# Where the input stage's buffers lie: gather buffers, tables and staging tiles first, the large inputs last

## The chip, the cores and the metric

The kernel runs on one core of a Trainium2 chip. The metric is device time in microseconds (us) of one execution of the whole program, the median of several runs. Lower is better. The engines are TensorE (PE), VectorE (DVE), ScalarE (ACT), GpSimd (POOL) and SyncE (SP, which here only issues DMAs). All of them work out of the on-chip memory SBUF: 128 partitions, in each of which a tile has an address in bytes.

## The reference, cut to what matters

One inference step of a two-layer hybrid decoder, for a prompt of 1024 tokens and eight single-token samples with a paged cache of 4096 rows each. What matters is layer 0: one input projection, whose columns go to a convolution branch and to a sparse attention with three branches, and the sample group's compressed cache, which is a weighted sum of 32 rows a block:

```python
h = x @ w_in                                             # 1032 rows of 1024, all columns
a_val, a_glu, z_a, q, kv6, g3, z_b = jnp.split(h, cuts, axis=-1)
u = a_val * jax.nn.sigmoid(a_glu)
c = lax.conv_general_dilated(ext, conv_w, (1,), 'VALID', ...) + conv_b
ya = jax.nn.silu(_layer_norm(c, cln_g, cln_b)) * jax.nn.silu(z_a)
...
blk = kv_cmp[:, :n_cmp * L_CMP].reshape(B, n_cmp, L_CMP, 2, KV_H, HD_B)   # samples: gathered by page
kc = jnp.einsum('bnlgd,lg->bngd', blk[:, :, :, 0], wk_cmp)
vc = jnp.einsum('bnlgd,lg->bngd', blk[:, :, :, 1], wv_cmp)
...
o = g[..., 0:1] * o_c + g[..., 1:2] * o_s + g[..., 2:3] * o_w   # compressed, selected, window
y = jnp.concatenate([ya, yb], axis=-1) @ w_out
```

Layer 1 is an RWKV-7 recurrence with its own projections, and each layer ends with a layer norm.

## The kernel before

The program has three stages that follow one another on PE.

**The input stage** (`phase_a`, L129, with `conv_norm`, L406) holds the input, 1032 columns by 1024, as a rounded part and a remainder (`xh`, `xl`: "hi" and "lo" parts, so that three fast matmuls stand for one exact one). For each block of 128 projection columns it loads weights `w` (L191, by SP), splits them into `wh` and `wl`, and runs 72 matmuls (L217 to L219). Beside that, as generators that are drawn on in turn, run the convolution and `cmp_task` (L239 to L260): 32 tasks, four for each sample. Each gathers 1 MB of cache pages into one of two buffers `cbuf` by an indirect DMA that POOL issues (L244), with row numbers from the table `cix` (made of `pti`, `ptf` and `cidx`). Three of four then scale the eight rows on ACT by the table `wrow` (L250, eight instructions), add them up on POOL in three steps of 1024, 512 and 256 elements (L252) and add the sum into `acc` on POOL (L253); the fourth does it all on DVE (L258, L260). The last three tasks reach past the last projection matmul. `tmp` (four buffers) stages the input at the start and gate values later; `c` is the convolution's output, `U0` and `U1` its inputs, `cw`, `cvec`, `wcT` and `US` its tables and the samples' states.

**Attention** (`phase_b`, L441) takes the prompt in eight tiles of 128 queries. Two sets of query tiles, `Q[u, 1]` and `Q[u, 2]`, are used in turn. To make a tile, SP loads `qt` (L476) and `zt` (L478), POOL loads two position rows into `Q[u, 2]` (L480), DVE casts the rounded part (L484), ACT copies (L485) and POOL subtracts the remainder (L486); ACT has zeroed part of `Q[u, 2]` once (L466). PE then runs the scores of the compressed (`Kc`), selected (`Ks`) and window (`Kw`) branches (L470), with masks added by a further matmul (L558). The masks `mdiag`, `mfar` come by way of the two staging buffers `PT` (L454, cast at L456), the mask `mcmp` directly (L459). ACT takes the exponentials `Ps` and `Pw` (L567), PE transposes them (L590) and multiplies by the values (L619, L621). The samples' attention (`sample_b`, L746) is worked in between: a cleared tile `QQ` (L764) filled by 16 small copies (L774), transposed compressed keys `KcT` (L808, L811), and 32-column score matmuls (L817).

**The recurrence** is layer 1; its weights, among them `w_out` (L1015), are loaded by SP too.

What sets the order: the code is written in the order of the stages, and a scheduler reorders it for each engine by priority and readiness; it also inserts the waits. Memory is given out by pools: each pool is a contiguous stretch of the partition, and the pools of `phase_a` follow one another in the order in which they are opened. When `phase_a` closes its pools, `phase_b` opens its own over the same bytes. A tile of attention may be written only when the work on all tiles of the input stage that lay under it is over, tile by tile (`reuse_waits="tile"`). So the order of pools in one stage decides what the next stage's tiles wait for. In bytes per partition, from 70,304 on, the input stage lies so: `xh`, `xl` to 136,352; `wh`, `wl` to 152,736; then `c`, the tables, `w`, `U0`, `U1` and more; `tmp` at 187,872; `cbuf` from 204,384 to 220,768. Attention's tiles are, from the same start: the masks to 71,840; the four `Q` tiles 71,872 to 88,256; `PT` to 92,352; `qt` to 96,448; `zt` to 100,544; and on. The samples' tiles come from the other end: `QQ` at 196,736 to 204,928, `KcT` from 207,264.

Of the kernel before, what the change touches and what calls it, by code (L numbers as in the profile page):

```python
# [8 lines left out]
F32 = mybir.dt.float32  # L9
F32R = mybir.dt.float32r  # L10
BF = mybir.dt.bfloat16
I32 = mybir.dt.int32
U32 = mybir.dt.uint32
# [8 lines left out]
NS = 8  # L22
# [3 lines left out]
CW = 31  # L26
# [102 lines left out]
def phase_a(nc, tc, I, O, G, es):  # L129
# [18 lines left out]
    G.acc = kp.tile([128, NS, 4, 64], F32, name="acc")  # L148
    with ExitStack() as ea:
        pool = lambda name, bufs, **k: ea.enter_context(tc.tile_pool(name=name, bufs=bufs, **k))  # L150
        xpl = pool("ax", 1)
        xh = xpl.tile([128, 8, TT], F32R, name="xh")
        xl = xpl.tile([128, 8, TT], F32R, name="xl")
        wp = pool("aw", 2)
        one = pool("a1", 1)
        tp = pool("at", 4)
        cp_ = pool("acmp", 2)
        ps, ps1 = G.ps, G.ps1
        c = one.tile([128, 4, TT], F32, name="c")
        zc = one.tile([64, 1], F32, name="zc")  # L160
# [13 lines left out]
        def build_k(nm, src, w):  # L174
            for g in range(2):
# [2 lines left out]
                nc.scalar.activation(k1[0:64], s, AF.Copy)  # L178
                nc.vector.tensor_copy(k1[64:128], s)
                nc.gpsimd.tensor_tensor(k2[64:128], s, k1[g * 64:g * 64 + 64], op=SUB)  # L180
        cw = one.tile([128, 4, CW], F32, name="cw")
        cwh = cw
        cvec = one.tile([128, 4, 3], F32, name="cvec")
        wcT = one.tile([128, 2, 32], F32, name="wcT")
        US = one.tile([128, 4, NS, CW], F32, name="US")

        def wload(i):
            n = 24 if FM[i][0] == "g3" else 128
# [18 lines left out]
        for i in range(4):  # L207
            nc.sync.dma_start(US[:, i, :, 0:CW - 1], I["conv_state"][:, i])
        nc.vector.tensor_scalar(cwh, cw, 0.5, None, op0=MUL)
# [12 lines left out]

        v2 = lambda t, lo, hi: t[:, lo:hi].rearrange("p (h n) -> p h n", n=NCK)
        U = {}
        pti = one.tile([128, NS], I32, name="pti")
        nc.sync.dma_start(pti, I["pt4"])
        wrow = one.tile([128, 32], F32, name="wrow")
        nc.sync.dma_start(wrow, I["wrow"])
        o, n_ = G.offd["cidx"]
        cidx = one.tile([128, 4], F32, name="cidx")  # L230
        nc.sync.dma_start(cidx, I["cstd"][:, o:o + n_])
        ptf = one.tile([128, NS], F32, name="ptf")
        nc.vector.tensor_copy(ptf, pti)
        nc.vector.tensor_scalar(ptf, ptf, 16.0, None, op0=MUL)
        cix = one.tile([128, NS, 4], U32, name="cix")
        nc.vector.tensor_tensor(cix, ptf.unsqueeze(2).to_broadcast([128, NS, 4]),
                                cidx.unsqueeze(1).to_broadcast([128, NS, 4]), op=ADD)

# [25 lines left out]
        def conv(i, e):  # L264
            u = U[i]
            e.tensor_scalar(c[:, i, 0:T], u[:, 0:T], cwh[:, i, 0:1], cvec[:, i, 0:1], op0=MUL, op1=ADD)
            for k in range(1, CW):
                e.scalar_tensor_tensor(c[:, i, 0:T], u[:, k:k + T], cwh[:, i, k:k + 1], c[:, i, 0:T],  # L268
                                       op0=MUL, op1=ADD)
                yield 1.15  # L270
            nc.scalar.dma_start(O["conv_s"][:, i], US[:, i, :, 1:CW])
            t = tp.tile([128, TT], F32, name="tmp")
            nc.vector.tensor_scalar(t[:, T - CW:T - 1], u[:, T:T + CW - 1], 0.5, None, op0=MUL)
            nc.scalar.dma_start(O["conv_p"][:, i], t[:, T - CW:T - 1])
            tv = t[:, 0:NS * CW].rearrange("p (b k) -> p b k", b=NS)
            nc.vector.tensor_tensor(tv, US[:, i], cw[:, i].unsqueeze(1).to_broadcast([128, NS, CW]), op=MUL)
            nc.vector.reduce_sum(c[:, i, T:TT], tv, axis=AX.X)
            nc.vector.tensor_scalar(c[:, i, T:TT], c[:, i, T:TT], 2.0, cvec[:, i, 0:1], op0=MUL, op1=ADD)
            yield 1.0
# [29 lines left out]
        for i, (kind, j) in enumerate(FM):  # L309
# [14 lines left out]
            if kind == "a":  # L324
# [7 lines left out]
                nc.vector.scalar_tensor_tensor(u[:, CW - 1 + lo:], th[:, lo:T], 1.0, s[:, 0:T - lo], op0=ADD, op1=MUL)  # L332
                nc.vector.scalar_tensor_tensor(US[:, j, :, CW - 1], th[:, T:TT], 1.0, s[:, T - lo:], op0=ADD, op1=MUL)
                nc.vector.tensor_scalar(US[:, j, :, CW - 1], US[:, j, :, CW - 1], 0.5, None, op0=MUL)
                fl.append(conv(j, nc.vector))
# [1515 lines left out]
def body(tc, I, O, stage="all"):  # L1851
# [4 lines left out]
    with ExitStack() as es:  # L1856
# [15 lines left out]
        with ExitStack() as eC:  # L1872
            G.eC = eC
            G.ps = eC.enter_context(tc.tile_pool(name="ps", bufs=2, space=PSUM))
            G.ps1 = eC.enter_context(tc.tile_pool(name="ps1", bufs=1, space=PSUM))
            with ExitStack() as e0:
                G.keepB = e0.enter_context(tc.tile_pool(name="keepB", bufs=1))
                phase_a(nc, tc, I, O, G, e0)
                if stage == "A":
                    nc.sync.dma_start(O["d_ya"], G.scr["ya"])  # L1880
                    nc.sync.dma_start(O["d_zb"][:, :, 0:T], G.scr["zb"][:, :, 0:T])
                    nc.sync.dma_start(O["d_zb"][:, :, T:], G.zs)
                    nc.sync.dma_start(O["d_qc"][:, :, 0:T], G.scr["q"][:, :, 0:T])
                    nc.sync.dma_start(O["d_qc"][:, :, T:], G.qs)
                    return
                phase_b(nc, tc, I, O, G)
                if stage in "BS":
                    nc.sync.dma_start(O["d_zb"], G.scr["yb"])
                    return
            phase_c(nc, tc, I, O, G)  # L1890
# [87 lines left out]
```

## Time and profile before

| | us |
|---|---|
| median of 3 runs | 2210.73 |
| lowest and highest | 2203.44, 2210.95 |
| the profiled execution, its own time | 2201.91 |
| its span, first to last instruction | 2200.2 |
| input stage, to PE's last projection matmul | 0 to 422.8 |
| PE without work between input stage and attention | 422.8 to 446.8 |
| attention on PE | 446.8 to 884 |
| recurrence and end | 884 to 2200 |

The profile is one execution on the chip. Its page gives each engine's busy time; the windows cut the span into stretches and give for each engine the busy time and the number of instructions, PE's granted clock (1.00 is 2.4 GHz, 0.50 is 1.2 GHz) and the share of DMA in use. The timeline lists instructions of one engine in order of start, those of the same kind together ("x3"), and behind them in brackets how long the engine stood idle before and what released it. "PEld" are PE's weight loads, "SPq" is SP's queue of DMA issues.

### The profile page before, as it was taken

How to read it: one execution, taken by the hardware profiler on the slowest of the kernel's cores; microseconds unless marked ns; L12 is line 12 of the kernel's file. 1: busy time of each engine (PE TensorE's matmuls, PEld its weight loads, DVE VectorE, ACT ScalarE, POOL GpSimd, SP SyncE). 2: the span in 40 equal slices, each digit the busy share in tenths (PEclk: the TensorE clock that was granted, in tenths of full speed). 3: DMA queues.
4: the chain of work that ended last, by engine and by line, in shares of the span. 5: the costliest groups of instructions: out<-in, count | busy, mean ns of one | idle time of the engine just before them, and what ended most of it. 6: DMA issues, size and time to landing. Idle time of an engine off the chain costs nothing. (4 is left out here: it accounts for less than half of the span.)

```text
span 2200.2 us, 41365 instructions
## 1 busy us (share of the span) xinstructions
PE 1844.0 (84%) x16026; PEld 1545.8 (70%) x16026; DVE 1491.9 (68%) x2543; ACT 1153.6 (52%) x2359; POOL 972.8 (44%) x784
## 2 busy tenths in 40 slices
PE   5988897668999997897887999897999787987865
PEld 5987896656767886674777987695888666875543
DVE  5998995557788878226364378827748987387453
ACT  3323324544665545357466467747754575465344
POOL 4667667554655545445345212323334434113233
PEclk9998998867999876898898999897899986988956
DMA  6424344521221213546556344433544544353333
GB/s 240 132 72 142 131 151 154 200 74 33 65 59 50 58 34 97 175 126 210 167 179 204 126 118 116 145 100 117 149 130 121 180 115 135 97 155 115 119 112 103
DMA packets 232095, 275.27 MB, mean 125 GB/s; under 512 B 71545, under 2 KB 171569, under 8 KB 227738
## 3 DMA queue, kind: packets, MB, share of 16 engines
q1 hardware_dynamic: 210712, 215.21, 32.1%
q0 software_dynamic: 7616, 41.52, 5.6%
q10 hardware_dynamic: 13570, 15.90, 2.0%
q8 instruction: 126, 2.06, 0.4%
q14 instruction: 71, 0.58, 0.1%
HBM read 212.47 MB, written 64.27 MB: 126 GB/s over the span
## 5 line engine op out<-in xcount | busy, mean ns | idle before, releaser
L121 POOL TENSOR_TENSOR wl<-w,wh 128x1024 fp32r<-128x1024 f32 x81 | 200.2, 2473 | 333.5 <-ACT wh L113 317.8
L1184 PE MATMUL mm<-xh,wh 128*128 128x256 f32 (+1 forms) x1024 | 308.3, 302 | 22.6 <-ACT og L1319 9.3
L1185 PE MATMUL mm<-xl,wh 128*128 128x256 f32 (+1 forms) x1024 | 300.9, 294 | 2.0 <-POOL xl L1212 1.1
L1186 PE MATMUL mm<-xh,wl 128*128 128x256 f32 (+1 forms) x1024 | 298.5, 293 | 3.5 <-POOL wl L121 3.5
L113 ACT ACTIVATE wh<-w 128x1024 fp32r<-128x1024 f32 (+2 forms) x130 | 134.4, 1036 | 208.2 <-PE mm L1185 60.9
L1184 PEld LDWEIGHTS mm<-xh,wh 128*128 128x128 f32 x1024 | 201.9, 198 | 35.8 <-ACT og L1319 12.0
L1185 PEld LDWEIGHTS mm<-xl,wh 128*128 128x128 f32 x1024 | 203.2, 198 | 5.4 <-issue 2.0
L1186 PEld LDWEIGHTS mm<-xh,wl 128*128 128x128 f32 x1024 | 202.1, 198 | 6.3 <-POOL wl L121 4.4
L268 DVE SCALAR_TENSOR_TENSOR c<-U,cw,c 128x1024 f32<-128x1024 f32 x120 | 198.0, 1674 | 0.9
L604 POOL TENSOR_TENSOR Pl<-PT,Ph 128x512 fp32r<-128x512 f32 (+1 forms) x102 | 131.9, 1298 | 150.4 <-DVE Ph L603 123.9
L252 POOL TENSOR_TENSOR cbuf<-cbuf 128x256 f32<-128x256 f32 (+2 forms) x72 | 131.3, 1829 | 85.2 <-ACT cbuf L250 82.3
L217 PE MATMUL S<-xh,wh 128*128 128x344 f32 (+1 forms) x432 | 146.6, 339 | 21.1 <-ACT wh L113 19.4
L219 PE MATMUL S<-xh,wl 128*128 128x344 f32 (+1 forms) x432 | 145.4, 337 | 15.7 <-POOL wl L121 11.6
L218 PE MATMUL S<-xl,wh 128*128 128x344 f32 (+1 forms) x432 | 146.3, 339 | 3.8 <-POOL xl L121 3.6
L1212 POOL TENSOR_TENSOR xl<-xs,xh 128x520 fp32r<-128x520 f32 (+1 forms) x76 | 104.6, 1382 | 91.2 <-ACT xh L1211 89.1
L250 ACT ACTIVATE cbuf<-cbuf,wrow 128x256 f32<-128x256 f32 x192 | 79.3, 496 | 112.1 <-DMA cbuf<-in_ccmp,cix 70.3
L1208 DVE SCALAR_TENSOR_TENSOR xs<-xk,mu,xs 128x512 f32<-128x512 f32 x96 | 92.7, 973 | 56.4 <-ACT xs L1207 55.7
L217 PEld LDWEIGHTS S<-xh,wh 128*128 128x128 f32 (+1 forms) x432 | 85.6, 198 | 23.2 <-ACT wh L113 21.9
L562 DVE TENSOR_REDUCE nm<-S 128x1 f32<-128x640 f32 (+7 forms) x128 | 88.3, 699 | 18.9 <-PE S L558 17.7
L219 PEld LDWEIGHTS S<-xh,wl 128*128 128x128 f32 (+1 forms) x432 | 84.9, 197 | 20.1 <-POOL wl L121 13.6
L121 DVE TENSOR_TENSOR wl<-w,wh 128x1024 fp32r<-128x1024 f32 x45 | 60.4, 1341 | 54.1 <-ACT wh L113 53.9
L218 PEld LDWEIGHTS S<-xl,wh 128*128 128x128 f32 (+1 forms) x432 | 84.8, 196 | 7.1 <-POOL xl L121 4.4
(610 smaller groups left out, 5399.3 us busy)
## 6 DMA issues: line engine op xcount, KB each, us to landing
w<-in_w_rkvz SPq DMA_DIRECT2D x64, 512.0 KB
w<-in_w_out SPq DMA_DIRECT2D x36, 512.0 KB
w<-in_w_fm SPq DMA_DIRECT2D x25, 512.0 KB
xk<-x1T SPq DMA_DIRECT2D x48, 260.0 KB
xk<-x1T SPq DMA_DIRECT2D x48, 256.0 KB
w<-in_w_out SPq DMA_DIRECT2D x16, 256.0 KB
x<-in_xp SPq DMA_DIRECT2D x8, 512.0 KB
x<-x ACTq DMA_DIRECT2D x8, 512.0 KB
```

The lines of the kernel that those rows point to most:

```text
L113: nc.scalar.activation(hi, src, AF.Copy, **({} if scale is None else {"scale": scale}))
L121: e_lo.tensor_tensor(lo, src, hi, op=SUB)
L217: nc.tensor.matmul(dst, lhsT=wh[:, k, 0:n], rhs=xh[:, k, sl], start=k == 0, stop=False)
L218: nc.tensor.matmul(dst, lhsT=wh[:, k, 0:n], rhs=xl[:, k, sl], start=False, stop=False)
L219: nc.tensor.matmul(dst, lhsT=wl[:, k, 0:n], rhs=xh[:, k, sl], start=False, stop=k == 7)
L252: nc.gpsimd.tensor_tensor(bv[:, 0:n], bv[:, 0:n], bv[:, n:2 * n], op=ADD)
L268: e.scalar_tensor_tensor(c[:, i, 0:T], u[:, k:k + T], cwh[:, i, k:k + 1], c[:, i, 0:T], op0=MUL, op1=ADD)
L604: lambda: nc.gpsimd.tensor_tensor(Pl[:, 0:w], PT[:, 0:w], Ph[:, 0:w], op=SUB)]
L1184: nc.tensor.matmul(dst, lhsT=wh[:, k], rhs=xh[k][:, lo:hi], start=k == 0, stop=False)
L1185: nc.tensor.matmul(dst, lhsT=wh[:, k], rhs=xl[k][:, lo:hi], start=False, stop=False)
L1186: nc.tensor.matmul(dst, lhsT=wl[:, k], rhs=xh[k][:, lo:hi], start=False, stop=k == 7)
L1212: (nc.vector if early[0] and k % LD == 0 else nc.gpsimd).tensor_tensor(lo[k][:, 0:n], t[:, 0:n], hi[k][:, 0:n], op=SUB)
```

## The change

In `phase_a` the order in which pools are opened changes. The gather buffers (`cp_`) come first, then a new pool `two`, then `tmp` (`tp`), and only then `xh` and `xl`, the weight pool and the pool `one`. Eight tables and states go from `one` to `two`: `cw`, `wcT`, `US`, `pti`, `wrow`, `cidx`, `ptf` and `cix`. Nothing else is edited. The lines of the kernel after stand one further down from L182 on.

```diff
--- before.py
+++ after.py
@@ -148,13 +148,14 @@
     G.acc = kp.tile([128, NS, 4, 64], F32, name="acc")
     with ExitStack() as ea:
         pool = lambda name, bufs, **k: ea.enter_context(tc.tile_pool(name=name, bufs=bufs, **k))
+        cp_ = pool("acmp", 2)
+        two = pool("a0", 1)
+        tp = pool("at", 4)
         xpl = pool("ax", 1)
         xh = xpl.tile([128, 8, TT], F32R, name="xh")
         xl = xpl.tile([128, 8, TT], F32R, name="xl")
         wp = pool("aw", 2)
         one = pool("a1", 1)
-        tp = pool("at", 4)
-        cp_ = pool("acmp", 2)
         ps, ps1 = G.ps, G.ps1
         c = one.tile([128, 4, TT], F32, name="c")
         zc = one.tile([64, 1], F32, name="zc")
@@ -178,11 +179,11 @@
                 nc.scalar.activation(k1[0:64], s, AF.Copy)
                 nc.vector.tensor_copy(k1[64:128], s)
                 nc.gpsimd.tensor_tensor(k2[64:128], s, k1[g * 64:g * 64 + 64], op=SUB)
-        cw = one.tile([128, 4, CW], F32, name="cw")
+        cw = two.tile([128, 4, CW], F32, name="cw")
         cwh = cw
         cvec = one.tile([128, 4, 3], F32, name="cvec")
-        wcT = one.tile([128, 2, 32], F32, name="wcT")
-        US = one.tile([128, 4, NS, CW], F32, name="US")
+        wcT = two.tile([128, 2, 32], F32, name="wcT")
+        US = two.tile([128, 4, NS, CW], F32, name="US")
 
         def wload(i):
             n = 24 if FM[i][0] == "g3" else 128
@@ -222,17 +223,17 @@
 
         v2 = lambda t, lo, hi: t[:, lo:hi].rearrange("p (h n) -> p h n", n=NCK)
         U = {}
-        pti = one.tile([128, NS], I32, name="pti")
+        pti = two.tile([128, NS], I32, name="pti")
         nc.sync.dma_start(pti, I["pt4"])
-        wrow = one.tile([128, 32], F32, name="wrow")
+        wrow = two.tile([128, 32], F32, name="wrow")
         nc.sync.dma_start(wrow, I["wrow"])
         o, n_ = G.offd["cidx"]
-        cidx = one.tile([128, 4], F32, name="cidx")
+        cidx = two.tile([128, 4], F32, name="cidx")
         nc.sync.dma_start(cidx, I["cstd"][:, o:o + n_])
-        ptf = one.tile([128, NS], F32, name="ptf")
+        ptf = two.tile([128, NS], F32, name="ptf")
         nc.vector.tensor_copy(ptf, pti)
         nc.vector.tensor_scalar(ptf, ptf, 16.0, None, op0=MUL)
-        cix = one.tile([128, NS, 4], U32, name="cix")
+        cix = two.tile([128, NS, 4], U32, name="cix")
         nc.vector.tensor_tensor(cix, ptf.unsqueeze(2).to_broadcast([128, NS, 4]),
                                 cidx.unsqueeze(1).to_broadcast([128, NS, 4]), op=ADD)
 
```

In bytes per partition the input stage then lies so: `cbuf` 70,304 to 86,688; `cw`, `wcT`, `US` to 91,424; `pti`, `wrow`, `cidx`, `ptf`, `cix` to 91,776; `tmp` to 108,288; `xh`, `xl` to 174,336; `wh`, `wl` to 190,720; `c` to 207,232; then the rest to 219,864 and beyond. Attention's tiles and the samples' lie where they lay. So the masks and `Q` now share bytes with `cbuf`, `cw`, `wcT` and `US` instead of `xh`; `PT` with `US`, the small tables and one `tmp`; `qt` and `zt` with `tmp`; `QQ` and `KcT` with `c` and `w` instead of `tmp` and `cbuf`.

The program has the same instructions as before. Up to the last projection matmul each engine's order is the same too; from there on the scheduler orders the passage to attention otherwise.

SP, from the last weights of the input projection on. `PT`, `mcmp` are masks, `qt`, `zt` the loads of a query tile, `w<-in_w_out` weights of the output projection, `cd` and `pti` tables of the samples' attention. Before:

```order
L191 DMA w<-in_w_fm 128x1024 x16
L454 DMA PT<-in_cstb 128x128 x2
L459 DMA mcmp<-in_cstb 128x256
L476 DMA qt<-q 128x4x128
L478 DMA zt<-zb 128x4x128
L476 DMA qt<-q 128x4x128
L478 DMA zt<-zb 128x4x128
L476 DMA qt<-q 128x4x128 x2
L1015 DMA w<-in_w_out 128x512 x3
L758 DMA cd<-in_cstd 128x482
L844 DMA pti_3793<-in_pt 16x32
```

After:

```order
L192 DMA w<-in_w_fm 128x1024 x16
L1016 DMA w<-in_w_out 128x512 x3
L759 DMA cd<-in_cstd 128x482
L845 DMA pti_3797<-in_pt 16x32
L455 DMA PT<-in_cstb 128x128 x2
L477 DMA qt<-q 128x4x128
L479 DMA zt<-zb 128x4x128
L477 DMA qt<-q 128x4x128
L479 DMA zt<-zb 128x4x128
L460 DMA mcmp<-in_cstb 128x256
L477 DMA qt<-q 128x4x128 x3
```

The loads of `w_out`, `cd` and `pti` moved from behind four query loads to the front, and `mcmp` from ahead of the query loads to behind two of them.

POOL, from the last but one gather (L244; after: L245) to the last piece of the first two query tiles. `Q_3331`, `Q_3332` are the two parts of one query tile and `Q_3334`, `Q_3335` of the next (after: 3335, 3336, 3338, 3339). Before:

```order
L244 DMA cbuf<-in_ccmp,cix 128x2048
L480 DMA Q_3332<-in_qaug 2x1024
L480 DMA Q_3335<-in_qaug 2x1024
L252 TENSOR_TENSOR cbuf<-cbuf 128x1024
L252 TENSOR_TENSOR cbuf<-cbuf 128x512
L486 TENSOR_TENSOR Q_3331<-qt,Q_3331 64x512
L252 TENSOR_TENSOR cbuf<-cbuf 128x1024
L252 TENSOR_TENSOR cbuf<-cbuf 128x256
L486 TENSOR_TENSOR Q_3331<-qt,Q_3332 64x512
L486 TENSOR_TENSOR Q_3334<-qt,Q_3334 64x512
L486 TENSOR_TENSOR Q_3334<-qt,Q_3335 64x512
```

After, from the last gather on:

```order
L245 DMA cbuf<-in_ccmp,cix 128x2048
L253 TENSOR_TENSOR cbuf<-cbuf 128x256
L254 TENSOR_TENSOR acc<-acc,cbuf 128x256
L253 TENSOR_TENSOR cbuf<-cbuf 128x1024
L253 TENSOR_TENSOR cbuf<-cbuf 128x512
L253 TENSOR_TENSOR cbuf<-cbuf 128x256
L254 TENSOR_TENSOR acc<-acc,cbuf 128x256
L462 MEMSET zc 64x1
L487 TENSOR_TENSOR Q_3335<-qt,Q_3335 64x512
L487 TENSOR_TENSOR Q_3335<-qt,Q_3336 64x512
L487 TENSOR_TENSOR Q_3338<-qt,Q_3338 64x512
L481 DMA Q_3336<-in_qaug 2x1024
```

Before, the first four subtractions of Q stand between the additions of the last-but-one tasks, and the last gather stands behind them; after, all tasks are added up first, and Q, with its loads of position rows, stands behind the last `acc`.

ACT, from the last gate copy of the input stage (L323; after: L324) to the first exponential. Before:

```order
L323 ACTIVATE tmp<-mm 128x344
L466 ACTIVATE Q_3332<-zc 64x1024
L466 ACTIVATE Q_3335<-zc 64x1024
L350 DMA za<-tmp 128x1032
L437 DMA ya<-c 128x1032
L250 ACTIVATE cbuf<-cbuf,wrow 128x256 x16
L485 ACTIVATE Q_3332<-qt 64x512 x2
L485 ACTIVATE Q_3335<-qt 64x512 x2
L567 ACTIVATE Ps,RS<-S,nm 128x1024
```

After:

```order
L324 ACTIVATE tmp<-mm 128x344
L351 DMA za<-tmp 128x1032
L438 DMA ya<-c 128x1032
L251 ACTIVATE cbuf<-cbuf,wrow 128x256 x16
L775 ACTIVATE QQ<-qs 64x8 x16
L251 ACTIVATE cbuf<-cbuf,wrow 128x256 x8
L486 ACTIVATE Q_3336<-qt 64x512 x2
L486 ACTIVATE Q_3339<-qt 64x512
L467 ACTIVATE Q_3336<-zc 64x1024
L467 ACTIVATE Q_3339<-zc 64x1024
L486 ACTIVATE Q_3339<-qt 64x512
```

The zeroing of `Q` (L466) moved from ahead of the last 24 scalings to behind them, and the samples' `QQ` copies (L774) came ahead of `Q`.

## Rows read from the trace of the kernel before

**Rows 1.** The page, section 1: busy time and share of PE.

```profile
PE 1844.0 (84%) x16026; PEld 1545.8 (70%) x16026; DVE 1491.9 (68%) x2543; ACT 1153.6 (52%) x2359; POOL 972.8 (44%) x784
```

**Rows 2.** Windows: stretch, busy (count) of PE, PEld, DVE, ACT, POOL; clock, DMA.

```profile
425.00:445.00 20.00, 0.00 (x0) 0.00 (x0) 11.90 (x19) 10.14 (x20) 12.67 (x12) 0.56 0.88 302
445.00:460.00 15.00, 11.45 (x39) 8.55 (x40) 8.78 (x18) 7.21 (x14) 12.06 (x11) 0.50 0.42 132
465.00:475.00 10.00, 5.77 (x17) 3.84 (x17) 5.12 (x9) 8.64 (x19) 4.92 (x4) 0.50 0.01 2
485.00:505.00 20.00, 19.35 (x93) 19.38 (x93) 5.27 (x22) 5.24 (x16) 1.27 (x1) 0.51 0.00 1
446.80:884.00 437.20, 383.17 (x2583) 308.37 (x2583) 350.08 (x773) 240.10 (x558) 227.88 (x195) 0.83 0.19 56
```

**Rows 3.** Timeline of PE: start, length, line, operation [idle <-releaser].

```profile
446.80 0.39 PE L470 MATMUL mm<-Kc,Q 128*128 128x32 f32 x1 [23.96 <-ACT Q L485]
...
494.00 1.33 PE L817 MATMUL ac<-KcT,QQ 128*128 128x32 f32 x6
...
505.81 1.11 PE L590 MATMUL mm<-ident,Pw 128*128 128x128 f32 x4
```

**Rows 4.** What PE waited for, 446.9 to 505.9: total, times, longest.

```profile
PE S L470 <- ACT Pw L567: 8.9, 2, 6.2
PE ac L817 <- ACT KcT L811: 2.1, 1, 2.1
...
PE mm L470 <- POOL Q L486: 0.6, 1, 0.6
```

**Rows 5.** Timeline of ACT, same columns: scaling of page buffers.

```profile
442.80 3.30 ACT L250 ACTIVATE cbuf<-cbuf,wrow 128x256 f32<-128x256 f32 x8 [2.27 <-DMA cbuf<-in_ccmp,cix]
...
465.11 3.30 ACT L250 ACTIVATE cbuf<-cbuf,wrow 128x256 f32<-128x256 f32 x8 [6.35 <-DMA cbuf<-in_ccmp,cix]
```

**Rows 6.** POOL by group and shape, 425 to 480: busy, mean ns.

```profile
L252 POOL TENSOR_TENSOR cbuf<-cbuf 128x1024 f32<-128x1024 f32 x4 | 9.4, 2349 | 21.1 <-ACT cbuf L250 20.5 <-POOL Q L486 0.6
L252 POOL TENSOR_TENSOR cbuf<-cbuf 128x512 f32<-128x512 f32 x4 | 5.1, 1264 | 0.2
...
L253 POOL TENSOR_TENSOR acc<-acc,cbuf 128x256 f32<-128x256 f32 x4 | 3.3, 828 | 0.2
...
L252 POOL TENSOR_TENSOR cbuf<-cbuf 128x256 f32<-128x256 f32 x4 | 3.2, 789 | 0.1
...
L764 POOL MEMSET QQ<- 128x2048 f32 x1 | 2.2, 2233 | 0.1
```

**Rows 7.** Timeline of POOL: issue of the last gather.

```profile
456.37 1.01 POOL L244 DMA_INDIRECT cbuf<-in_ccmp,cix  x1 [0.16 <-POOL cbuf L252]
```

**Rows 8.** All 32 gathers (L244), then the three from 420 on.

```profile
DMA to landing us min/median/max: 5.4/7.1/20.2
...
DMA to landing us min/median/max: 5.6/7.9/8.6
```

**Rows 9.** Timeline of SP: a query load, the w_out loads.

```profile
437.18 0.52 SPq L476 DMA_DIRECT2D qt<-q  x1
...
453.95 1.51 SPq L1015 DMA_DIRECT2D w<-in_w_out  x3
```

**Rows 10.** Timeline of DVE: Q casts that waited for it.

```profile
444.73 1.63 DVE L484 CAST Q<-qt 64x512 fp32r<-64x512 f32 x2 [6.85 <-DMA qt<-q]
```

**Rows 11.** The small load of position rows (L480).

```profile
DMA to landing us min/median/max: 1.9/2.1/6.9
```

**Rows 12.** Tile Q: its makers, duration ns min/median/max, first and last start.

```profile
L484 DVE CAST Q<-qt x16: 408/424/1453, 437.0 to 808.7; 64x512 fp32r<-64x512 f32 x16
L486 POOL TENSOR_TENSOR Q<-qt,Q x16: 1258/1267/1476, 444.4 to 807.2; 64x512 fp32r<-64x512 f32 x16
L485 ACT ACTIVATE Q<-qt x16: 627/628/632, 446.1 to 805.6; 64x512 fp32r<-64x512 f32 x16
...
L466 ACT ACTIVATE Q<-zc x2: 1042/1042/1043, 434.3 to 435.3; 64x1024 fp32r<-64x1024 f32 x2
```

## The prediction

> **What bounds the kernel now.** The page first: TensorE (PE) is busy 84% of the span [rows 1], so the place to look is not its work but the holes in it. The windows then show a hole that this change can touch: from 425 to 445 us PE does nothing, and the stretches behind it run mostly at the lower clock, 0.50 [rows 2]. PE's own timeline gives the edge: the first score matmul starts at 446.80, after 23.96 us idle that ended on ACT's Q (L485) [rows 3]. So the passage from the input stage to attention is bound by the making of Q. ACT shows what is still at work there: the last-but-one page buffer is scaled from 442.80 on, the last only from 465.11 [rows 5], 18 us into attention, its gather having gone out at 456.37 [rows 7]. Q was zeroed at 434.3 and its pieces made between [rows 12]. That overlap is what the change touches.
>
> **The change part by part.** Nothing is added or removed: every tile, instruction and DMA of the input stage is there, in the same order up to its last matmul (PE, ACT, DVE, POOL and SP stand as before until then). I cost the new addresses themselves at nothing: ACT's zeroing takes 1042 or 1043 ns in either of two Q tiles that lie 8 KB apart, and its copies 627 to 632 ns in 16 [rows 12]. What moves is at the seam. Attention's Q tiles lay under xh, free after the last matmul, at 446.80 - 23.96 = 422.8 [rows 3]. Now they lie under the two gather buffers and US, the masks' first staging under US and the second under wrow, cix and a tmp. So Q, the masks and, on SP behind them, the query loads now wait for the last gather's work.
>
> *Restart of PE.* I follow the new order with the durations of before. ACT has scaled the first of the three late buffers at 442.80 - 2.27 = 440.5 and the second at 442.80 + 3.30 = 446.1 [rows 5]. POOL's additions take 2.35, 1.26 and 0.79, the one into acc 0.83 [rows 6]. So the first buffer is added up at 444.9; the second's first addition ends at 448.5, acc at 449.3, the QQ memset (2.23 [rows 6]), now ahead, at 451.5, the 512-wide addition at 452.8. Then the last gather is issued: 3.6 us earlier than before [rows 7], since no Q step stands between. From issue to landing the 32 gathers took 5.4 to 20.2, median 7.1; the three in this stretch took 5.6, 7.9 and 8.6 [rows 8], the last beside the three w_out loads issued at 453.95 [rows 9], which now go out long before. I take 7.1, and 5.6 and 8.6 as ends: landed at 459.9. Eight scalings (3.30) end at 463.2 and free wrow, so SP's second mask load and the query loads follow. The additions on the last buffer (2.35 + 1.26 + 0.79 + 0.83) end at 468.4; only then may Q be written. The query load has 5 us to land by then; the one before that was waited for took from 437.18 to 444.73, 7.6 us, under two gathers [rows 9, 10], so the high end gets 3 us more. For the mask's and the first Q's casts on DVE (0.42 for Q [rows 12]) I allow 0.6 together: 469.0. Three POOL subtractions (1.27 [rows 12]) end at 472.8, and POOL's small load of the position rows, in the order behind them, lands 2.1 later [rows 11]. ACT's part (three copies of 0.63 and two zeroings of 1.04 [rows 12]) ends at 472.4, within this. **PE restarts at 474.9 instead of 446.80: 28.1 us later** (26.6 with the short gather, 32.6 with the long one and the slow query load).
>
> The Trainium skill, in DMA: Bandwidth & Descriptors, section Bandwidth, measured a 1 MB load issued from GpSimd at 6.15 us, below this trace's median of 7.1 for the same kind of load; by it the last gather would land 1 us sooner, and the sum below would be 11 and not 12.
>
> *What is caught up.* From the restart to the first Pw transpose at 505.81, the point where both orders meet again, before needs 59.0 us [rows 3]. Three waits make up 11.6 of it: 8.9 for ACT's Pw exponential in two, the longest 6.2; 2.1 for KcT on ACT; 0.6 for POOL's Q [rows 4]. The 6.2 us are a Pw in ACT's queue behind the last buffer's scaling, which waited 6.35 for its gather [rows 5]; KcT stands behind the QQ copies. After the change the gather, the scaling, all of Q, the QQ memset and copies are done before PE restarts, so 6.2 + 2.1 + 0.6 = 8.9 us go and 50.1 stay. The rest depends on the clock. In the trace PE ran at half (0.50) from 445 to 460, 465 to 475 and 485 to 505 [rows 2]; between, I take it as full. If the new stretch copied those halves, it would take 50. If all were at full: the half-clock PE time is 11.45 + 5.77 + 19.35 = 36.6 us, half of which would go, leaving 32. In between: the first 15 us after a hole at half, as here; the block of 32-column matmuls from 494.00 to 505.81 [rows 3] at half, as here; the denser score work from 469 to 474 and 486 to 494 (13 us) at full, since no gap of 6.2 or 2.1 precedes it. That saves 6.5: 43.6, rounded to **43 us, so 16 of the 28 come back**.
>
> The Trainium skill, in TensorE: Matmul & The Clock Gate, section Part 1: The HAM clock gate, holds that the throttled clock is the default and that activity releases it. The trace does not bear that out for the 20 us from 485 on, where PE is busy all the time at 0.50 [rows 2]. By the page the late stretch, which has no holes, would all be at the higher level and take 32; that is the first rival below.
>
> *Behind 505.81* the order differs in pieces to the end of the program (loads of w_out, Q's later parts, DMAs of the recurrence), with the same instructions. The trace has no row for it; the nearest is one such pair of waits, of scores for ACT's Pw, 8.9 us [rows 4]: about 8 more or fewer, of either sign; I take 0. Attention has no hole in which a late start could vanish: from 446.8 to 884 PE is busy 383 of 437 us [rows 2].
>
> **Sum:** 28.1 - 16 + 0 = **+12 us**. On the profiled execution's own 2201.91 (span 2200.2 and 1.7 around it) that is 2214. That execution lies below the three runs (2203.44, 2210.73, 2210.95), so on the median I forecast **2223**. About 0.5%, 11 us, is what a measurement of this kernel can tell from no change; the forecast stands at that edge.
>
> **The rivals.**
> - *Not slower: the late start runs uninterrupted at full clock.* Price: the stretch takes 32 and not 43, so +1, 2212; together with a lucky order behind it, down to 2204. For it: all inputs are ready, and PE is not at half everywhere: from 446.8 to 884 the clock is 0.83 [rows 2]. Against: from 485 to 505 it was at half without a gap [rows 2]. It decides if PE has the full clock from 10 us after its restart on.
> - *The loss stays whole.* Half clock throughout and first-unit softmax waits that were hidden under Q's slow making: the stretch takes 50 or more, +19 to +28, 2230 to 2239. For it: the first two pairs of scores now come at once and wait for one exponential after the other. Against: DVE, ACT and POOL bring less other work.
> - *The move has no effect,* because the last gather's work comes so early that Q need not wait: 2211. Against: the second late buffer is scaled only at 446.1, by its own gather [rows 5], and the last gather waits for its additions, so that one can't land before 458.
>
> **How the numbers follow.** Forecast (+4 to +19): 0.52. Not slower by the clock: 0.24. Loss whole: 0.18. No effect: 0.06. The range takes in both ends of restart and stretch (26.6 - 27 = 0 to 32.6 - 9 = +24, where 27 = 59 - 32 and 9 = 59 - 50) and part of the 8 us of order: 2206 to 2238. Slower by over 0.5%: the loss whole and somewhat over half of the forecast, 0.48. Faster by over 0.5%: the clock rival with a better order, 0.10. Within: 0.42. Here most of the chance holds one sign; the forecast's own range is 2215 to 2230.
>
> **What would show it.** After: a PE hole from 422.5 to some 475, ended by POOL's load of Q's position rows (or POOL's Q); the last gather issued near 453 and scaled by 463; SP's second mask load and the query loads waiting until then; no 6.2 us wait for Pw afterwards; the first Pw transpose near 518, 12 us late, and the end of attention late by the same. Wrong would be: a restart before 465 (a wait that I read into the order isn't there), a first Pw transpose before 509 or after 527 (the clock, or the softmax of the first units), or an attention and recurrence stage that differs by over 8 us in themselves (the order behind the seam).

## The result, and the profile after

| | before | after |
|---|---|---|
| median of 4 runs, us | 2210.84 | 2185.28 |
| lowest and highest | 2203.44, 2213.54 | 2175.84, 2191.91 |
| the profiled execution, its own time | 2201.91 | 2191.91 |

The ratio is 0.9893, with a 95% interval from 0.9862 to 0.9925: the change makes the kernel 1.1% faster (24 us), where 2223, a small loss, was forecast. The time lies below the whole range.

From the page of after, the span and the engines' busy times (answers to [rows 1]):

```profile
span 2190.1 us, 41396 instructions
PE 1819.0 (83%) x16026; PEld 1528.8 (70%) x16026; DVE 1491.1 (68%) x2543; ACT 1153.9 (53%) x2359; POOL 976.3 (45%) x784
```

PE's busy time is 25 us less than in [rows 1], for the same 16026 matmuls and a span 10 us shorter: PE's idle time over the span did not shrink, the same matmuls took less time. PE's granted clock, 0.871 over the span before and 0.876 after, has a part in this.

**The seam went as worked out.** PE's timeline of after, answering to [rows 3], shows the restart, the block of 32-column matmuls and the first Pw transpose:

```profile
474.84 3.56 PE L471 MATMUL mm<-Kc,Q 128*128 128x32 f32 x16 [51.27 <-DMA Q<-in_qaug]
...
500.72 4.69 PE L818 MATMUL ac<-KcT,QQ 128*128 128x32 f32 x40
...
508.63 1.11 PE L591 MATMUL mm<-ident,Pw 128*128 128x128 f32 x4
```

What stands ahead of that restart, on POOL (answers to [rows 6, 7, 12]):

```profile
453.13 0.95 POOL L245 DMA_INDIRECT cbuf<-in_ccmp,cix  x1
...
462.37 4.48 POOL L253 TENSOR_TENSOR cbuf<-cbuf 128x1024 f32<-128x1024 f32 x3 [6.72 <-ACT cbuf L251]
...
468.45 4.31 POOL L487 TENSOR_TENSOR Q<-qt,Q 64x512 fp32r<-64x512 f32 x3 [0.65 <-DVE Q L485]
472.71 1.10 POOL L481 DMA_DIRECT2D Q<-in_qaug  x2
```

on ACT (answers to [rows 5]):

```profile
458.99 3.30 ACT L251 ACTIVATE cbuf<-cbuf,wrow 128x256 f32<-128x256 f32 x8 [3.60 <-DMA cbuf<-in_ccmp,cix]
467.68 1.92 ACT L486 ACTIVATE Q<-qt 64x512 fp32r<-64x512 f32 x3 [5.39 <-POOL acc L254]
```

and in SP's queue (answers to [rows 9]):

```profile
446.01 16.63 SPq L455 DMA_DIRECT2D PT<-in_cstb  x2
462.69 0.55 SPq L477 DMA_DIRECT2D qt<-q  x1
```

Read together: the last gather goes out at 453.13, is scaled from 458.99 to 462.3, SP's second mask load sits in the queue until then and the query loads behind it, POOL's last additions end at 467.65, and Q is made only from there. POOL's small load of position rows releases PE at 474.84.

PE's clock behind the restart, in windows of after with the columns of [rows 2]: between its two levels at first, then full for 20 us of nearly unbroken work, then at half for 5 us that are no less busy:

```profile
474.80:485.00 10.20, 8.99 (x49) 7.03 (x50) 5.83 (x13) 2.84 (x6) 0.34 (x1) 0.69 0.10 27
485.00:505.00 20.00, 19.74 (x145) 16.41 (x145) 16.13 (x32) 13.46 (x31) 4.26 (x3) 1.00 0.01 2
505.00:510.00 5.00, 5.00 (x26) 5.00 (x26) 3.82 (x18) 0.59 (x3) 0.00 (x0) 0.51 0.00 0
```

PE's waits of after from 475 to 508, answering to [rows 4]; the 6.2 us and the 2.1 us are gone:

```profile
PE mm L471 <- DMA Q<-in_qaug: 51.3, 1, 51.3
PE S L471 <- ACT Ps L568: 1.1, 1, 1.1
```

**Where the gain comes from.** Some matmuls stand at the same place of PE's order in both programs, with the same instructions ahead and behind. Their starts in the two traces:

| PE reaches | before | after | difference |
|---|---|---|---|
| restart | 446.8 | 474.8 | +28.0 |
| first Pw transpose | 505.8 | 508.6 | +2.8 |
| a point early in attention | 569.3 | 568.8 | -0.5 |
| attention's second half, start | 670.5 | 670.0 | -0.5 |
| attention's second half, end | 916.7 | 925.0 | +8.3 |
| a point in the recurrence | 1428.4 | 1437.3 | +8.9 |
| the next, "first stretch" ends | 1718.4 | 1714.0 | -4.4 |
| the next, "second stretch" ends | 1897.0 | 1885.7 | -11.3 |
| end of the span | 2200.2 | 2190.1 | -10.1 |

So in this pair of traces nearly all of the loss at the seam is given back 34 us behind the restart, and the gain arises some 950 us further on, in two stretches of the recurrence that do the same work in another order. The windows of these two stretches and, ahead of them, of attention's second half, before:

```profile
670.50:916.70 246.20, 216.85 (x1515) 179.73 (x1514) 186.93 (x416) 125.68 (x307) 122.60 (x103) 0.79 0.28 80
1428.40:1718.40 290.00, 263.70 (x3216) 227.04 (x3217) 181.49 (x323) 168.37 (x358) 99.99 (x96) 0.90 0.42 125
1718.40:1897.00 178.60, 149.24 (x1759) 119.10 (x1755) 133.80 (x252) 104.03 (x205) 67.12 (x56) 0.84 0.44 135
```

and after:

```profile
670.00:925.00 255.00, 222.59 (x1515) 182.48 (x1514) 181.69 (x416) 126.36 (x306) 121.56 (x103) 0.77 0.27 77
1437.30:1714.00 276.70, 259.51 (x3216) 225.39 (x3216) 184.78 (x324) 167.15 (x358) 104.18 (x96) 0.92 0.44 132
1714.00:1885.70 171.70, 138.73 (x1759) 111.67 (x1755) 131.09 (x249) 103.17 (x205) 72.47 (x56) 0.86 0.45 139
```

The first stretch loses 13.3 us: stretch less PE's busy time is PE's idle time, 26.3 before and 17.2 after, so 9.1 of idle, and 4.2 of PE's busy time. The second loses 6.9, and there the busy time falls by 10.5 at a higher clock while the idle time rises by 3.6.

### The profile page after: what moved, and what is told of

The parts are those of the page before. It is cut to its first block, busy times and chain, and to the rows that moved or that the text cites. A ratio compares the mean times of both kernels' runs of the same rounds, so it can differ in the third digit from the quotient of the medians.

```text
span 2190.1 us, 41396 instructions
## 1 busy us (share of the span) xinstructions
PE 1819.0 (83%) x16026; PEld 1528.8 (70%) x16026; DVE 1491.1 (68%) x2543; ACT 1153.9 (53%) x2359; POOL 976.3 (45%) x784
## 5 line engine op out<-in xcount | busy, mean ns | idle before, releaser
L253 POOL TENSOR_TENSOR cbuf<-cbuf 128x1024 f32<-128x1024 f32 (+2 forms) x72 | 130.4, 1817 | 85.2 <-ACT cbuf L251 82.9
L1209 DVE SCALAR_TENSOR_TENSOR xs<-xk,mu,xs 128x512 f32<-128x512 f32 x96 | 93.3, 976 | 52.7 <-ACT xs L1208 51.4
```

The lines of the kernel that those rows point to most:

```text
L253: nc.gpsimd.tensor_tensor(bv[:, 0:n], bv[:, 0:n], bv[:, n:2 * n], op=ADD)
```

## The experiments

The code gives a reason why the order so far behind the seam moves at all: the scheduler orders by a timeline that it simulates for itself, so a Q that comes later there shifts what it holds to be ready from then on. That is read from the code. Whether the order is what counts, and not the addresses, is a question for the chip. The tool for it is a function that runs after the program is written, and before the scheduler orders it. From a table it takes, for each engine, which instruction is to follow which, and adds an order-only dependency between them (no semaphore, no wait):

```diff
+def in_order(tc, nc):
+    ...
+                if prev is not None:
+                    tc.add_manual_dep(ins, prev.name, mybir.DependencyInfo(
+                        mybir.DependencyClass.NoSync, mybir.DependencyReason.DATA), reason="order")
+                prev = ins
     with tile.TileContext(nc, schedule_with_timeline_sim=True) as tc:
         body(tc, I, O)
+        in_order(tc, nc)
```

The tables cover only what lies behind a place in mid-attention, up to which both programs have worked off the same instructions. Ratios are to the kernel before, each with its 95% interval; its median was 2208 in these comparisons.

**Seam or order.** Four kernels: after itself; after with before's order behind the seam; before with after's order behind the seam; after with before's order in attention's second half alone. The edit to each but the first, which is after unchanged, is the function above with its table.

> The kernel after, unchanged, timed once more on the chip that the three runs below share, so that they can be read against it. In its first profile the seam had cost nothing any more 100 us behind it (-0.5 us at 550), attention ended 8 us late, and the recurrence won 18 us back. Both theories expect a ratio of 0.989 to before, about 2185.

> The addresses and the seam of after, but from the middle of attention on every engine has its instructions in the order of the kernel before. Theory ORDER: the new addresses and the late Q are worth nothing, the whole gain is the other order of the recurrence; this run then loses the gain, 2207 to 2214, ratio 0.998 to 1.002. Rival SEAM: the gain comes from the seam or from where the tiles lie; this run keeps it, 2180 to 2190, ratio 0.986 to 0.991.

> The reverse: addresses and seam of before, and from the middle of attention on the order of the kernel after. Theory ORDER: it has the whole gain, 2180 to 2190, ratio 0.986 to 0.991. Rival SEAM: it has none, 2207 to 2214, ratio 0.998 to 1.002.

> The kernel after, with the second half of attention alone put back into the order of before; the recurrence keeps the order of after. By the traces the new order of attention costs 8 us by its end. If that is a loss of its own: 8 us less than after, about 2177, ratio 0.985. If the recurrence would have waited anyway, it is as after, 2185, ratio 0.989.

| kernel | addresses and seam | order behind | median us | ratio |
|---|---|---|---|---|
| after_again | after | after | 2184.18 | 0.9907 [0.9873, 0.9940] |
| seam_only | after | before | 2211.06 | 1.0020 [0.9993, 1.0047] |
| order_only | before | after | 2175.73 | 0.9870 [0.9820, 0.9920] |
| attention_of_before | after | before's in attention's second half | 2190.78 | 0.9929 [0.9898, 0.9959] |

The gain goes with the order. With after's addresses and before's order nothing is left of it; with before's addresses and after's order it is all there. Both kernels carry the function, so the function itself isn't the gain. The two stretches in the trace of seam_only:

```profile
1445.30:1733.00 287.70, 261.17 (x3215) 225.25 (x3214) 180.95 (x325) 168.19 (x359) 101.44 (x98) 0.91 0.41 127
1733.00:1912.70 179.70, 150.94 (x1759) 120.35 (x1755) 131.86 (x249) 103.77 (x205) 65.64 (x55) 0.83 0.43 132
```

and of order_only:

```profile
1428.80:1706.20 277.40, 258.98 (x3216) 224.97 (x3214) 178.09 (x323) 166.96 (x358) 105.87 (x96) 0.92 0.43 132
1706.20:1878.10 171.90, 140.59 (x1759) 113.53 (x1755) 131.20 (x249) 103.10 (x205) 71.70 (x56) 0.85 0.45 138
```

287.7 and 179.7 are before's lengths, 277.4 and 171.9 are after's. The 8.8 us by which attention's second half was longer in after's first trace are no loss of its order: with before's order there, the kernel is not faster than after. It met neither forecast (0.985 or 0.989), and its interval overlaps after's. In 14 traces that half took 239 to 258 us, with much scatter under either order: 246.2, 255.4, 252.0, 252.7, 249.0 and 257.9 in before's, 255.0, 242.9, 255.5, 243.2, 239.4 and 249.6 in after's, 239.5 and 242.4 in two that the scheduler ordered by itself. PE's idle time in it hardly differs (29.4 in before's trace, 32.4 in after's); most of the scatter goes with the granted clock, from 0.76 to 0.85. The mean is 252.2 us for the six with before's order and 245.9 for the other eight: a few us of gain may lie here too, but the scatter doesn't settle it.

**Which stretch.** Before with after's order in the first stretch alone, and in the second alone (same function, shorter tables).

> Addresses, seam and order of before, except for one stretch of the recurrence (about 1430 to 1660 us), where every engine takes the order of after. In three traces with that order this stretch is 12 us shorter, in two without it not. Theory ADD (each stretch has its own gain): 2196, ratio 0.993 to 0.996. Rival JOINT (the gain is there only if the later stretch is ordered to match, since it waits for the same end): 2208, ratio 0.998 to 1.002.

> The same for the later stretch alone (about 1715 to 1900 us), which is 7 us shorter in the traces with the order of after. Theory ADD: 2201, ratio 0.995 to 0.998. Rival JOINT: 2208, ratio 0.999 to 1.002, or slower, since the work that was to be earlier is not.

first_only: 2193.07 us, 0.9944 [0.9917, 0.9971], so 12.4 us. second_only: 2204.27 us, 0.9983 [0.9959, 1.0006], some 4 us, in which no gain at all is still possible. In the trace of first_only only its stretch is short:

```profile
1438.90:1715.70 276.80, 259.93 (x3215) 225.57 (x3214) 182.39 (x323) 166.92 (x358) 105.10 (x96) 0.92 0.43 132
1715.70:1894.60 178.90, 149.33 (x1758) 119.19 (x1754) 134.53 (x252) 103.94 (x205) 67.32 (x56) 0.84 0.43 133
```

and in second_only's only the other:

```profile
1434.40:1722.20 287.80, 263.14 (x3215) 226.41 (x3216) 181.59 (x324) 168.19 (x358) 101.34 (x96) 0.90 0.41 127
1722.20:1893.60 171.40, 142.44 (x1758) 114.76 (x1754) 131.58 (x249) 103.27 (x205) 71.06 (x56) 0.84 0.45 140
```

By the traces each gain stands on its own; added up they are 12.4 + 3.7 = 16 timed, where the second isn't clear of zero, and 13 + 7 = 20 by the first pair of traces. Over all traces the two orders lie apart in both stretches. The first took 276.7 to 282.8 us in seven with after's order and 287.7 to 290.0 in four with before's, in the mean 10 us apart; the second took 171.2 to 172.3 us in nine and 178.6 to 179.7 in four.

**Which edit of the layout.** Before with the gather buffers' pool alone moved to the front, and with the staging tiles' pool (`tmp`) alone moved there.

```diff
         pool = lambda name, bufs, **k: ea.enter_context(tc.tile_pool(name=name, bufs=bufs, **k))
+        cp_ = pool("acmp", 2)
         xpl = pool("ax", 1)
...
         tp = pool("at", 4)
-        cp_ = pool("acmp", 2)
```

> A part of the change alone: the gather buffers are laid out first, tables and staging tiles stay behind. Q then lies under the gather buffers as in after, so the seam should be as late as there, PE restarting at 470 to 478. Its recurrence comes out in the order of after in both stretches, without any order forced. Theory ORDER: as after, 2180 to 2190, ratio 0.986 to 0.992. If the tables mattered too: in between, 2195 to 2205.

```diff
         pool = lambda name, bufs, **k: ea.enter_context(tc.tile_pool(name=name, bufs=bufs, **k))
+        tp = pool("at", 4)
         xpl = pool("ax", 1)
...
         one = pool("a1", 1)
-        tp = pool("at", 4)
```

> Another layout: only the four staging tiles tmp are laid out first, so Q lies under them and need not wait for the last gather; PE should restart at 447 to 455, as before. The recurrence comes out in a third order that is neither that of before nor that of after. If the seam decided: 2205 to 2215, ratio 0.998 to 1.002. Theory ORDER makes no forecast of the sign, only that what the time differs from 2208 by arises in the recurrence; 2175 to 2235.

gather_buffers_first: 2187.13 us, 0.9912 [0.9884, 0.9940]. staging_first: 2184.36 us, 0.9892 [0.9856, 0.9928]. PE's restart in the one and in the other, from their timelines:

```profile
478.26 3.57 PE L470 MATMUL mm<-Kc,Q 128*128 128x32 f32 x16 [52.50 <-DMA Q<-in_qaug]
```

```profile
456.38 3.56 PE L470 MATMUL mm<-Kc,Q 128*128 128x32 f32 x16 [29.85 <-DMA Q<-in_qaug]
```

The gather buffers alone make the whole late restart, and the scheduler gives that kernel after's order in both stretches by itself (282.8 and 171.5 us). The staging tiles alone make a restart 9.6 us later, a little past the 447 to 455 expected, and a third order. Its second stretch takes 179.0 us, like before's. Its first stretch can't be cut as above, since this order has done other matmuls by the place where it begins in the others; read from the last place ahead that it shares with before's, over the same matmuls up to the stretch's end, before takes 323.7 us (1394.7 to 1718.4) and staging_first 319.4 (1380.4 to 1699.8), a gain of only 4. Where most of the 24 us by which staging_first is timed faster arises isn't shown. Four layouts, three orders behind the seam: none of that is in the diff.

**The layout of staging_first under either order.** If its gain is its order's, it must go when before's order is put behind it.

> The layout with the four staging tiles first, its own passage into attention, and from the middle of attention on the order of before. Its first profile was 8 us ahead of before at 570 us, but two other runs with the passage of before were 3 and 8 ahead there too. If the passage is worth nothing: 2205 to 2211, ratio 0.998 to 1.002, and the whole gain of that layout was its third order of the recurrence. If it is worth the 8 us: 2200, ratio 0.996.

> The same layout and passage, and from the middle of attention on the order of after: the best of both if the parts add. Order alone gave 0.987 with the passage of before. If the passage is worth nothing: 0.985 to 0.990, 2176 to 2186. If it is worth 8 us: 0.983, 2171.

staging_before_order: 2202.78 us, 0.9983 [0.9962, 1.0004]. staging_after_order: 2177.29 us, 0.9876 [0.9848, 0.9904]. So with before's order the layout is worth some 4 us, by its interval perhaps nothing (between the two forecasts), and the rest of its own gain goes with its order behind the middle of attention; with after's order it has the whole gain. Of the kernels here order_only and staging_after_order are the lowest. Both beat before clearly; over after they are 0.3% ahead, and the intervals overlap, so that they beat after isn't settled.

**What in the order.** In the first stretch of before, PE's longest waits are for ACT's `og` and, among others, for the transposes of `U` by which `joinUT` (L1466) begins, a chain from PE to ACT to PE to DVE and back that joins the blocks of a triangular inverse:

```profile
PE mm L1294 <- ACT og L1296: 4.9, 1, 4.9
...
PE pg L1477 <- DVE U L1471: 2.0, 1, 2.0
```

DVE's timeline of before shows where one unit's join stands: its first transposes (L1471) come 35 us behind the unit before it (L1494), behind a run of elementwise work of another step:

```profile
1476.69 0.45 DVE L1494 STREAM_TRANSPOSE U<-UT 128x256 f32<-128x256 f32 x1
...
1507.04 0.68 DVE L1377 TENSOR_TENSOR AM<-rt,P 128x512 f32<-128x512 f32 x1
...
1512.09 0.45 DVE L1471 STREAM_TRANSPOSE U<-UT 128x256 f32<-128x256 f32 x1
```

After has it 4 us behind (lines one further down):

```profile
1485.30 0.45 DVE L1495 STREAM_TRANSPOSE U<-UT 128x256 f32<-128x256 f32 x1
1489.60 0.97 DVE L1472 STREAM_TRANSPOSE U<-UT 128x256 f32<-128x256 f32 x2 [3.85 <-PE pg L1501]
```

So join_late takes after and puts this one unit's join back to where before has it, on PE, ACT and DVE, and join_half half of the way (same function; the tables hold after's order with some 6 to 69 of PE's rows, 9 to 20 of ACT's and 8 to 26 of DVE's moved). The reverse, the early join alone put into before, wasn't tried.

> The kernel after; every engine keeps its order, except that one step of the recurrence, the joining of one unit's inverse (DVE's transpose L1471 up to DVE's copy L1511: on PE, ACT and DVE), is put as far back among the other work as it stands in the kernel before: 6 to 69 rows on PE, 9 to 20 on ACT, 8 to 26 on DVE. Theory JOIN: this step's place is what the first stretch gains by, since in the traces its transposes run some 10 us later in before; 8 to 12 us lost, 2192 to 2197, ratio 0.993 to 0.997. Rival SPREAD: the gain is in many small places; 0 to 3 us lost, 2184 to 2188, ratio 0.989 to 0.992.

> The same step put back half as far. JOIN: 3 to 7 us lost, 2187 to 2192. SPREAD: as after, 2184 to 2187.

join_late: 2194.78 us, 0.9929 [0.9894, 0.9964]. join_half: 2187.0 us, 0.9909 [0.9875, 0.9943]. The first lies where the theory of the join put it, above after's 0.9907, and the second beside after; but all intervals overlap, so the times don't decide it. The trace of join_late does for the idle part. Its attention half and its first stretch:

```profile
669.50:908.90 239.40, 206.12 (x1515) 168.78 (x1514) 182.29 (x416) 124.94 (x306) 121.82 (x103) 0.84 0.28 82
1419.10:1704.40 285.30, 261.77 (x3216) 227.81 (x3215) 183.10 (x324) 167.25 (x358) 105.17 (x96) 0.91 0.41 128
```

and PE's waits in that stretch:

```profile
PE pg L1501 <- DVE U L1495: 3.9, 1, 3.9
...
PE pg L1509 <- ACT Gs L1504: 2.7, 1, 2.7
```

PE is idle for 285.3 - 261.8 = 23.5 us, after's 17.2 plus 6.3, and the two waits in the moved join make 6.6. In after's own stretch the second of them is 0.6:

```profile
PE pA L1522 <- DVE E L1530: 3.7, 2, 3.3
...
PE pg L1509 <- ACT Gs L1504: 0.6, 1, 0.6
```

So in after's order this join's place is worth some 6 us of PE's idle time: put late, two of its steps leave PE without other work. These are not the 9 us that before loses. There the moved join's wait for `U` is 2.0, and the longest wait is for ACT's `og`, 4.9 us. It is 4.9 to 6.2 in all four traces with before's order, and 0.3 at most in the seven with after's, in join_late and in join_half. ACT's timeline of before shows what stands ahead of that `og`:

```profile
1533.36 1.28 ACT L1351 ACT_TABLE_LOAD   x1
1534.66 0.69 ACT L1351 ACTIVATE inv<-sm,eps_kk 128x512 f32<-128x512 f32 x1
1535.36 1.28 ACT L1296 ACT_TABLE_LOAD   x1
1536.66 0.38 ACT L1296 ACTIVATE og<-mm 128x256 f32<-128x256 f32 x1
```

ACT spends twice 1.28 us on an ACT_TABLE_LOAD, ahead of `inv` and ahead of `og`, while PE stands idle until 1537.09. Three such loads stand at this `og` line in before's stretch and none in after's, with 20 in all in either. So the larger part of the idle time that after's order saves is, by the traces, ACT's order around `og`; no run moved that alone.

The half-way place of the join costs no idle time (16.0), yet its trace shows the longest first stretch of all, at a granted clock of 0.86:

```profile
1429.70:1721.80 292.10, 276.05 (x3216) 238.34 (x3217) 179.24 (x323) 167.40 (x358) 105.99 (x96) 0.86 0.40 126
```

PE's busy time makes the rest of the first gain and all of the second, and what sets it stays open. In the first stretch it doesn't part the orders: 259.0 to 265.3 us in seven traces with after's order, 261.2 to 264.9 in four with before's. There the idle time does, 16.3 to 18.4 us against 23.9 to 26.5. In the second it goes with the order, 139 to 143 us against 149 to 151, but the mean granted clock doesn't tell the two apart: first_only and second_only show 0.84 both, with 149.33 and 142.44 us.

## Why the prediction was wrong, point by point

- **Restart of PE: right.** 474.9 was worked out, 474.84 came, with the releaser that was named. Its steps: last gather out at 452.8, measured 453.13; scaled by 463.2, 462.3; added up by 468.4, 467.65; the three subtractions of Q took 4.31 for 3.81. That the sum hits to 0.1 us is in part luck: misses of up to 0.9 us cancel. The gather took less than the 7.1 us taken for it: from its issue to ACT's start behind it 458.99 - 453.13 = 5.9. The Trainium skill, DMA: Bandwidth & Descriptors, section Bandwidth, has 6.15 us for a 1 MB load. This gather lies nearer to that than to the median of the trace, but the page's figure counts the transfer alone, without the issuing that 5.9 and 7.1 have in them, so it isn't a test of it. Seven traces with gather buffers in front have the restart between 474.2 and 478.3.
- **What is caught up: the mechanism right, the size off.** From the restart to the first Pw transpose 43 us was forecast within 32 to 50; it took 33.8, and 32.9 to 34.0 in the other traces of that seam. The waits of 8.9 went as said. The mis-sized term is the clock: full from 485 to 505, so the rival "at full clock" held on its own point, 10 us after the restart. The Trainium skill's rule in TensorE: Matmul & The Clock Gate, section Part 1: The HAM clock gate, that activity releases the clock, was weighed against before's 20 us at 0.51 and lost; here the trace agrees with it from 485 to 505, and not from 505 to 510, at 0.51 with PE busy throughout. The baseline of 59.0 was another part of the error: before's seam took 49.9 in order_only's trace, 51.4 in first_only's and 58.1 in second_only's. The block of 32-column matmuls that begins at 494.00 in [rows 3] shows it. All of it, from the timelines of before, of order_only and of second_only, which have the same order there:

```profile
494.00 8.58 PE L817 MATMUL ac<-KcT,QQ 128*128 128x32 f32 x40
```

```profile
490.13 4.55 PE L817 MATMUL ac<-KcT,QQ 128*128 128x32 f32 x40
```

```profile
492.78 8.58 PE L817 MATMUL ac<-KcT,QQ 128*128 128x32 f32 x40
```

  It takes 8.58 us, to 502.58 and not to 505.81, or about half of that: one trace's clock was taken for a property of the place. With the late seam it took 4.60 to 4.70 us in all seven traces. What the seam costs in the end, seam_only tells: 0.2%, +4.4 us [-1.5, +10.4], where +12 was forecast. The traces agree: where before stands at 569.3, early in attention, four kernels with before's seam stand at 561 to 569, mean 565, seven with after's at 567.5 to 572.7, mean 570. Of 28 us, then, 24 are caught up and not 16.
- **"Behind 505.81 ... 0, about 8 more or fewer": the step that failed.** The order behind the seam is worth 13 + 7 = 20 us by the traces (12.4 + 3.7 timed), all of the gain and more. With the seam that makes -20 + 4 = -16; timed were -24 ± 7 in the result and -20.5 ± 7 in after_again, and order_only's -29 ± 11 is likewise more than its traced -20, so some of the gain has no sure place in these traces; attention's second half may hold a few us of it. The bound of 8 was one pair of waits in attention. But the order differed to the end of the program, and the holes that it could fill stood in the trace of before: 26.3 us of PE's idle time and a clock of 0.90 in the first stretch, 29.4 us and 0.84 in the second. The idle time alone gives a bound of 26.3 + 29.4 = 56 us, and not 8; and the second stretch gained without losing idle time at all.
- **The rivals.** "Not slower by the clock" named the right mechanism at the seam, but ended at 2212, with 2204 for a lucky order behind it. It allowed the order 8 us; the measured 2185 lies 27 below its 2212. "The loss stays whole" is refuted by the 33.8 us. "No effect" is refuted by the restart.
- **What would show it.** A hole to 475, the gather at 453, the waiting mask load, and no wait of 6.2: all seen. A first Pw transpose before 509, and a recurrence that differs by over 8 us in itself, had been named as what would be wrong: both came.

## What to carry to other kernels

When a scheduler orders the program, an edit of addresses is an edit of the order of everything behind it: compare the two orders to the end, and bound what that can bring by PE's idle time and half-clock work over the whole reordered part, not by the place of the edit. A layout's own worth is known only with the order held fixed; here the seam cost about 4 us and the order gained 20 or more, and an order can be kept without the layout. In the order, look for the few long waits that one order has and the other has not: here a wait of 5 to 6 us for ACT in before's, and, in join_late, 6 us at a chain of small steps from engine to engine that was moved to where PE had no other work.

## What the runs showed of the hardware

- **The same matmuls in the same order run at either clock level from run to run.** 40 matmuls of 32 columns took 8.58 us in two traces of before's seam (above) and 4.55 and 4.76 in two others. Attention's second half, in after's order both times, took 239.4 us at a granted clock of 0.84 in join_late and 255.0 at 0.77 in after (lines above), with nearly the same idle time on PE, 33.3 and 32.4 us.

- **The recurrence's second stretch doesn't scatter so.** Nine traces with after's order lie between 171.2 and 172.3 us, four with before's between 178.6 and 179.7, though neither PE's idle time parts them (29.4 in before's trace, 33.0 in after's) nor the mean granted clock (0.83 to 0.84 in the four, 0.84 to 0.86 in the nine). With its order given this stretch repeats within about 1 us, attention's half does not; why isn't known.
